# Moving the sine network of the Hyena filters to the head of the program, under raised priority

## The chip, the core and the metric

The kernel runs on one core of a Trainium2 chip. Five engines work side by side, each through its own list of instructions in a fixed order: PE (TensorE, matrix products), DVE (VectorE) and POOL (GpSimd) for element-wise work, ACT (ScalarE) for functions and copies, and SP (SyncE), which here only issues DMA transfers. The metric is the time of one execution on the device in microseconds (us), the median of several.

## The reference

One step of a two-layer model for 1024 tokens of a sample and 128 tokens of a prompt, 1024 channels wide. Layer 0 is a Hyena layer: a norm, shift and scale from a conditioning vector (adaLN), an input projection into x0, x1, v and a gate, a short convolution, a long convolution by Fourier transforms, an output projection. Layer 1 is latent attention with 16 heads. What the change touches is the small network that makes the filters of the long convolution:

```python
def hyena_filters(L, w1, b1, freq, w2, b2, w3):
    ...
    hdn = jnp.sin(fr * (z @ w1.astype(f32) + b1.astype(f32)))
    hdn = jnp.sin(fr * (hdn @ w2.astype(f32) + b2.astype(f32)))
    h = hdn @ w3.astype(f32)
    ...
    h = h * jnp.exp(-t * deltas)
    return h / jnp.sum(jnp.abs(h), axis=0, keepdims=True)
```

`z` depends on the position alone, and the hidden width is 64. So the two sine layers need nothing of the tokens, and the tokens need nothing of them until the filters are transformed. The rest that matters here:

```python
    hf = jnp.fft.rfft(filt, n=n, axis=0)
    ...
    y = jnp.fft.irfft(jnp.fft.rfft(z, n=n, axis=1) * hf, n=n, axis=1)[:, :L]
    y = (y + z * f_bias.astype(jnp.float32)).astype(h.dtype) * x0
    return (y * jax.nn.silu(gate)) @ w_out
```

## The kernel before, in words

Every float32 product is split into three with a high and a low part of each side (`_h`, `_l`), so a weight needs an ACT pass (`hi`, L86 to L93) and a POOL or DVE pass (`lo`, L94 to L96) before PE can use it.

The Hyena layer (`hyena`, from L654) runs in four stages.

1. **Start** (L680 to L739). Nine tiles of 128 tokens are loaded (`load_x`, L650), normed in thirds (squares L171 and root L172 on ACT, reciprocal L174 and scaling L176 on DVE), and turned by PE, three tiles at a time (`turn`, L178 to L182, 72 products of 128x128 into `sf_ps`, a tag with three PSUM buffers; ACT copies the result out at L700). Eight chunks of the adaLN weights, 1 MB each, go through PE (`ada_chunk`, L104 to L117) and are turned (`ada_turn`, L127). Then ACT applies shift and scale (`modulate`, L206), POOL and DVE split the result into `hT` and `lT` (L90, L96), and PE makes the first two of 30 blocks of the input projection in 144 products (L726), whose accumulators are three `ip_ps` and the three `sf_ps` buffers. The **sine network** (`filters`, L235 to L252) is written between the turning and these products. Its two layers (`sin_layer`, L211 to L225) each go in columns of 512, 512 and 128: a PE product into `sf_ps` (L215), a chain of seven DVE instructions that reduces the argument (L219 to L224), and the Sin on ACT (L225). The result is `hs`.
2. **Forward** (L740 to L762). For each of eight groups of 128 channels: the filter from `hs` (`group_filter`, L254), two blocks of the projection (`in_proj`, L404, 72 products each at L415), the short convolution (L435 to L443), the forward transform in PE products into `df_ps` (L357, L364, and L485 for the prompt) and the product with the filter, stored in DRAM. Between them lie 32 **chunks of the later adaLN weights** (`fill`, L753 to L755; four a group, L760), each in two halves with one buffer for the weights, turned at L127 or L142 and, for the gate rows, stored by POOL's queue (L146).
3. **Inverse** (L763 to L784). The inverse's constants `ic` and `ip` are loaded in the place that the filters' pool held, the pool of the weights of `fill` among it (`load_const`, L513 to L528, two buffers). Each group is read back, split (`pi_h` on ACT, `pi_l` on POOL), inverted by PE into `iv_ps` (L551), copied out by ACT (L553), put together by DVE (`ds`, `bf`, `yv`, L559 to L591) and stored (L784). Blocks of the projection that are left, for x0 and the gate, lie between (`PLAN`).
4. **Output** (from L785): the weights of `w_out` are loaded in the place of the constants, the eight results are read back (`y<-YD`, L792), split, and multiplied (L627).

The order on each engine is made by a scheduler from the written order: an instruction gets a priority by its place in the text, `urgent()` (L389) raises it by 3000 places, and of those that the scheduler's own model holds ready, the one of highest priority is put next. The lists are then fixed: an engine waits at the head of its list, even if later work is ready. The lines in question:

```python
                with self.urgent():
                    xs = [self.load_x(np_, t, NT + 1) for t in range(NT)]
                ...
                if FIRST == 1:
                    self.filters(fp, ps, hs)
                ...
                    with self.urgent():
                        for f in fill[4 * g:4 * g + 4]:
                            f()
```

Of the kernel before, what the change touches and what calls it, by code (L numbers as in the profile page):

```python
# [19 lines left out]
# channel groups whose x0 and gate are made along with a group's forward transform  # L20
GATES = (0, None, None, 1, None, None, None, None)
NY = 6          # channel groups inverted before the input projection ends
# [9 lines left out]
FIRST = 1  # L32
# [10 lines left out]
# the steps of a unit of attention (scores of the next one, transposes, products with the values)  # L43
# [10 lines left out]
NT = 9          # token tiles: 8 of the sample, 1 of the prompt  # L54
T = NT * P
EPS = 1e-6
# [13 lines left out]
# columns of the per-partition vector table  # L70
NK = 1408       # keys: 1024 of the sample, 256 of the cache, 128 of the prompt
# [4 lines left out]
class K:  # L76
# [8 lines left out]
    # hi = x rounded to float32r, lo = the exact rest  # L85
# [18 lines left out]
    # ---------------------------------------------------------------- adaLN  # L104
    def ada_chunk(self, layer, o, n, pool, ps, kk, bufs):
        """n columns from o of silu(cond) @ ada_w, as four partial sums on rows 32g + cond."""
# [12 lines left out]
    def ada_col(self, layer, m, o, n, pool, ps, kk, bufs):  # L119
        """columns o.. of shift and scale with the channel on the partition."""  # L120
        self.ada_turn(layer, m, o, n, self.ada_chunk(layer, o, n, pool, ps, kk, bufs), ps)
# [10 lines left out]
    def ada_mod(self, layer, m, A, k):  # L132
        """A = norm_w (1 + scale) for the channel tiles k."""
        c = C_NORM + 8 * layer
        nw = self.cols[:, c + k.start:c + k.stop].unsqueeze(2).broadcast_to([P, k.stop - k.start, 2])
        self.stt(A[:, k], m[:, 8 + k.start:8 + k.stop, :], 1.0, nw, ALU.mult, ALU.add)

    def ada_row(self, layer, gd, o, n, pool, ps, kk, bufs):
        """columns o.. of the gates as rows in DRAM."""
# [13 lines left out]
    # ------------------------------------------------- RMSNorm and modulate  # L153
# [11 lines left out]
    def norm(self, xs, ys, pool, eng=None):  # L165
        """ys = rmsnorm(xs) without its weight; the squares pass through ys, or a tile of their own."""
# [17 lines left out]
    def norm_mod(self, xs, tiles, pool, ps, A, B, hT, lT):  # L184
        """h^T (hi, lo): [128 channels, 8, tokens] of rmsnorm(x) * A + B, for neighbouring token tiles."""
# [12 lines left out]
    def modulate(self, x, k, c, pool, A, B):  # L198
        """x^T A + B for the channels k of the third c of the tokens."""
# [10 lines left out]
    # ------------------------------------------------------------- filters  # L210
    def sin_layer(self, pool, ps, w, src, kk, out, col):  # L211
        """out = sin(freq * (w^T src + b)) with the argument reduced to [-pi, pi]."""
# [14 lines left out]
    def load_w3(self, pool, g, bufs):  # L227
        """the last filter weights of 128 channels, forward and backward, on both halves of the rows."""
# [6 lines left out]
    def filters(self, pool, ps, hs):  # L235
        """hs: hidden features [hi; lo] by token."""
# [16 lines left out]
    # -------------------------------------------------------- long convolution  # L253
    def group_filter(self, g, q):  # L254
        """time-domain filter of 128 channels into the filter columns of E and O, and of the prompt."""
# [10 lines left out]
        # forward and backward taps: the sample at 0, the prompt at 1025, a zero behind each  # L266
# [9 lines left out]
        # the taps over the sums of their absolute values  # L276
# [11 lines left out]
        # sum and difference of the forward taps and the reversed backward ones  # L288
# [55 lines left out]
    def dft_tile(self, k0, ab, q):  # L344
        """the frequencies k0 + 16 m of z (columns 0:128) and of the filter (128:256)."""
# [22 lines left out]
    def product(self, pt, special, q, out):  # L368
        """out [128, 2, 128] = z * filter; special: row 0 holds two real frequencies."""
# [18 lines left out]
    # ------------------------------------------------------------ Hyena: in  # L388
# [15 lines left out]
    def in_proj(self, m, q, cb):  # L404
        """128 output channels of h @ hy_w_in; cb(psum, token offset)."""
# [16 lines left out]
    def conv_in(self, m, q):  # L422
        """one of x0, x1, v: projection, then the short convolution; [128, 1153] with column 1024 unused."""
# [21 lines left out]
    def hyena_group(self, g, q):  # L445
# [21 lines left out]
        # sample  # L467
# [7 lines left out]
        # prompt  # L475
# [54 lines left out]
    # ----------------------------------------------------------- Hyena: out  # L530
    def inverse(self, g, q):
        """y = irfft(product): [128 channels, T]."""
        nc, pool, ps = self.nc, q["pool"], q["ps"]
        ih, il, jh, jl = q["ih"], q["il"], q["jh"], q["jl"]
        # blocks 1 2 3 7 6 5 of (real, imaginary), and the blocks 0 (even, odd) and 4
# [22 lines left out]
        # d: W1 - W7, W2 - W6, W3 - W5 in blocks 0, 2, 4 (imaginary: 1, 3, 5), s: the sums in blocks 6..11  # L558
# [10 lines left out]
        # a0 a3 a2 a1 in blocks 0..3  # L569
# [22 lines left out]
        # prompt  # L592
# [17 lines left out]
    def load_w(self, src, pool, ncol, tag, bufs, raw_bufs=2, hi_eng="act", lo_eng="dve", lo_bufs=None, step=2, tag_raw="w_raw", size=None, stage=None):  # L610
        """a [128, kt, ncol] weight chunk, split."""
# [17 lines left out]
    # ------------------------------------------------------------------ run  # L629
# [25 lines left out]
    def hyena(self):  # L655
# [9 lines left out]
        # in thirds of the tokens: the first ones' place comes free before the last product ends  # L665
# [12 lines left out]
        with self.pool("hsp", side="right") as hp:  # L678
            hs = hp.tile([P, T], F32R, name="hs")
            q.update(hs=hs)  # L680
            with self.pool("fp", 2, side="right") as fp, self.pool("ap", side="right") as ap, \
# [3 lines left out]
                with self.urgent():  # L685
                    xs = [self.load_x(np_, t, NT + 1) for t in range(NT)]
                q["n"], q["w"] = 2, [self.in_weights(m, q) for m in q["order"][:2]]
                # the normed tokens with the channel on the partition: in places of the convolution's and of x
# [12 lines left out]
                if FIRST == 1:  # L701
                    self.filters(fp, ps, hs)
                # the first two projections, along the channels as they come
# [5 lines left out]
                # shift and scale of 256 channels at a time; a chunk is turned after the next one's products  # L709
# [19 lines left out]
                if FIRST == 2:  # L729
# [767 lines left out]
```

## Time and profile before

| | before |
|---|---|
| median of 3 runs | 1869.53 us (1867.89 to 1870.08) |
| profiled execution, first to last instruction | span 1868.4 us |
| PE busy | 1785.4 us (96%), 11480 products |
| DVE busy | 1291.5 us (69%) |
| ACT busy | 1116.4 us (60%) |
| POOL busy | 616.9 us (33%) |
| mean granted TensorE clock | 0.984 |
| DMA | 157.93 MB, mean 85 GB/s |

The profile has only the span of the profiled execution; the median is 1.1 us above it, and it is that execution's own time that the runs are compared by. Busy PE is not PE at its peak, since a product's end is modelled and overlaps the next one's start: distances between starts tell more. The shares are means over stages with different limits, so a stage is read by windows and by each engine's list in order of time.

### The profile page before, as it was taken

Reading aid. Unit: us, or ns where it says so; the run is one execution under the profiler, and the core shown is the slowest. Engines: PE = TensorE matmul, PEld = TensorE weight load, DVE = VectorE, ACT = ScalarE, POOL = GpSimd, SP = SyncE. Lnnn points to the kernel's source line nnn. Section 1 sums busy time; section 2 is a strip of 40 time slices with the busy share of each in tenths; the row PEclk is TensorE's granted clock in tenths of the full one; section 3 lists DMA queues with packets and bytes.
Section 4 is the critical chain, followed back from the end, with each engine's and each line's share of the span. In section 5 each row is a group of like instructions: output and inputs, shape, how many; then the busy total and the mean of one; then the engine's idle time right before and its main releaser. Section 6 shows DMA issues by size and latency. Waiting matters only on the chain.

```text
span 1868.4 us, 31762 instructions
## 1 busy us (share of the span) xinstructions
PE 1785.4 (96%) x11480; PEld 1585.0 (85%) x11480; DVE 1291.5 (69%) x2556; ACT 1116.4 (60%) x2650; POOL 616.9 (33%) x796
## 2 busy tenths in 40 slices
PE   6998999999999977999999989999999999999998
PEld 4887888887888877788999979999899998998786
DVE  3847887888865699753233268877887888778454
ACT  7655566665653443434353368878887888788431
POOL 2334433344345574233000042424343342235100
PEclk9999999999999988999999989999999999999999
DMA  8222232222223553731313410101010000012541
GB/s 316 83 84 72 66 94 93 82 82 66 74 95 112 168 167 103 279 134 65 94 33 109 102 31 19 42 16 46 20 37 28 20 28 24 18 35 62 180 134 68
DMA packets 126500, 157.93 MB, mean 85 GB/s; under 512 B 12711, under 2 KB 99687, under 8 KB 125064
## 3 DMA queue, kind: packets, MB, share of 16 engines
q1 hardware_dynamic: 123280, 152.51, 25.3%
q10 hardware_dynamic: 2552, 3.39, 0.6%
q8 instruction: 90, 1.47, 0.3%
q14 instruction: 66, 0.54, 0.1%
q0 software_dynamic: 512, 0.02, 0.0%
HBM read 113.89 MB, written 36.73 MB: 81 GB/s over the span
## 4 chain that ended last, share of the span: by engine, by line
PE 51%; DVE 5%; DMA 2%; ACT 1%; SPq 1%; issue 1%; POOL 0%; DVEq 0%; ACTq 0%; POOLq 0%
PE wo_ps L627 18%; PE wo_ps L1289 11%; PE av_ps L1174 8%; PE nm_ps L1162 7%; PE wo_ps L991 4%; PE nm_ps L1023 1%; DVE mx L1292 1%; DVE bf L99 1%; DMA og_in<-og 1%; SPq L978 1%; DMA y<-YD 0%; DVE kT L96 0%; PE nm_ps L842 0%; DMA wm_raw<-wm_a 0%; DVE yv L102 0%
## 5 line engine op out<-in xcount | busy, mean ns | idle before, releaser
L1289 PE MATMUL wo_ps<-kT,qT 128*128 128x512 f32 (+1 forms) x1152 | 281.4, 375 | 11.0 <-POOL qT L90 6.5
L1296 ACT ACTIVATE prob<-wo_ps,mx 128x512 f32<-128x512 f32 (+1 forms) x384 | 234.1, 618 | 22.9 <-DVE mx L1294 20.8
L1292 DVE TENSOR_REDUCE mx<-wo_ps 128x1 f32<-128x512 f32 (+1 forms) x384 | 213.0, 596 | 32.8 <-PE wo_ps L1289 32.1
L88 ACT ACTIVATE pt_h<-nm_ps 128x512 fp32r<-128x512 f32 x324 | 192.8, 599 | 70.4 <-PE nm_ps L1162 62.4
L1289 PEld LDWEIGHTS wo_ps<-kT,qT 128*128 128x128 f32 x1152 | 189.1, 191 | 46.4 <-ACT prob L1296 14.5
L96 DVE TENSOR_TENSOR pt_l<-nm_ps,pt_h 128x512 fp32r<-128x512 f32 x324 | 210.6, 683 | 13.0 <-ACT pt_h L88 12.8
L1162 PE MATMUL nm_ps<-ident,prob 128*128 128x128 f32 x1280 | 191.5, 272 | 0.0
L96 POOL TENSOR_TENSOR wi_l<-wi_raw,wi_h 128x512 fp32r<-128x512 f32 x64 | 127.3, 1989 | 185.1 <-ACT wi_h L88 181.7
L1162 PEld LDWEIGHTS nm_ps<-ident,prob 128*128 128x128 f32 x1280 | 150.0, 140 | 8.5
L415 PE MATMUL ip_ps<-lT,wi_h 128*128 128x384 f32 x720 | 157.1, 346 | 0.0
L415 PE MATMUL ip_ps<-hT,wi_l 128*128 128x384 f32 x720 | 152.8, 344 | 0.0
L415 PE MATMUL ip_ps<-hT,wi_h 128*128 128x384 f32 x720 | 152.5, 346 | 0.0
L1174 PE MATMUL av_ps<-pt_h,Vt 128*128 128x256 f32 x640 | 138.1, 297 | 0.0
L1174 PE MATMUL av_ps<-pt_l,Vt 128*128 128x256 f32 x640 | 135.4, 293 | 0.4 <-DVE pt_l L96 0.4
L415 PEld LDWEIGHTS ip_ps<-lT,wi_h 128*128 128x128 f32 x720 | 128.3, 192 | 6.7 <-issue 4.4
L415 PEld LDWEIGHTS ip_ps<-hT,wi_h 128*128 128x128 f32 x720 | 126.0, 190 | 6.4 <-issue 4.4
L415 PEld LDWEIGHTS ip_ps<-hT,wi_l 128*128 128x128 f32 x720 | 125.2, 189 | 7.1 <-issue 4.7
L627 PE MATMUL wo_ps<-wm_h,lhh 128*128 128x256 f32 (+1 forms) x432 | 126.5, 296 | 2.3 <-ACT wm_h L88 2.2
L1186 POOL TENSOR_SCALAR gt<-gt,sm 128x64 f32<-128x64 f32 x128 | 54.9, 443 | 220.6 <-DVE sm L1177 219.3
L627 PE MATMUL wo_ps<-wm_l,lhh 128*128 128x256 f32 (+1 forms) x432 | 127.1, 295 | 0.0
L627 PE MATMUL wo_ps<-wm_h,lhl 128*128 128x256 f32 (+1 forms) x432 | 126.7, 295 | 0.0
L99 POOL TENSOR_TENSOR pr<-ev 128x256 f32<-128x256 f32 x72 | 79.2, 1102 | 129.9 <-ACT ev L372 78.7
(354 smaller groups left out, 4348.2 us busy)
## 6 DMA issues: line engine op xcount, KB each, us to landing
wi_raw<-w_in SPq DMA_DIRECT2D x64, 256.0 KB, 3.0
ada_w<-ada_w SPq DMA_DIRECT2D x64, 256.0 KB, 2.8
x_in<-xs SPq DMA_DIRECT2D x16, 512.0 KB, 5.3
ada_w<-ada_w SPq DMA_DIRECT2D x8, 1024.0 KB
PS<-pr_o SPq DMA_DIRECT2D x64, 128.0 KB, 2.5
pi_raw<-PS SPq DMA_DIRECT2D x32, 256.0 KB, 3.6
YD<-yv SPq DMA_DIRECT2D x8, 576.0 KB, 4.5
y<-YD SPq DMA_DIRECT2D x8, 576.0 KB
```

The lines of the kernel that those rows point to most:

```text
L88: self.S.activation(out, src, AF.Copy)
L96: e.tensor_tensor(out, src, hi.bitcast(F32), ALU.subtract)
L99: (eng or self.V).tensor_tensor(out, x, y, op)
L415: mm = self.PE.matmul(pt, w[:, k, :], x[c][:, k, :], start=s == 0 and k == 0, stop=s == 2 and k == 7)
L627: self.PE.matmul(pt, x[k][:, sl], w[:, k, :], start=s == 0 and k == 0, stop=s == 2 and k == kt - 1)
L991: self.PE.matmul(pt[:, :n], x[:, k, o:o + P], y[:, k, c], start=s == 0 and k == 0, stop=s == 2 and k == kt - 1)
L1162: self.PE.transpose(pt[:, P * i:P * i + P], u["p"][i % 2][n // 2][:, P * (2 * (n % 2) + i // 2):P * (2 * (n % 2) + i // 2) + P], self.ident)
L1174: self.PE.matmul(u["po"][:, :256], m["V"][:, 2 * n + e, j, :], u[n][1 + s][:, 256 * e:256 * e + 256], start=n == first and e + s == 0, sto ...
L1186: self.G.tensor_scalar(o, o, u["sm"][:, i, 3:4], None, ALU.mult)
L1289: self.PE.matmul(pt[:, :n], x[:, j, P * i:P * i + P], y[:, j, o:o + n], start=s == 0, stop=s == 2)
L1292: self.V.tensor_reduce(mx[:, b:b + 1], c["s", i, b][:, :n], AX.X, ALU.max)
L1296: self.S.activation(c["p"][i][b], c["s", i, b][:, :n], AF.Exp, bias=c["mx"][i][:, 3:4], accum_out=c["sm"][:, i, b:b + 1])
```

## The change

`filters` is called first in the start stage, ahead of the token loads, and under `urgent()`; the call between the turning and the first products is taken out. Nothing that is computed changes. The comments and docstrings are taken out of the file too, which shifts line numbers by one to three (L726 before is L725 now) and leaves the program as it is.

```diff
-FIRST = 1
...
                 m0 = self.small.tile([P, 16, 2], F32, name="ada_m0")
                 with self.urgent():
+                    self.filters(fp, ps, hs)
+                with self.urgent():
                     xs = [self.load_x(np_, t, NT + 1) for t in range(NT)]
...
-                if FIRST == 1:
-                    self.filters(fp, ps, hs)
...
-                if FIRST == 2:
-                    self.filters(fp, ps, hs)
```

The scheduler makes other lists of it, down to the start of the output stage. Three places of them follow.

**PE at the start.** `zt`, `w` and `h` are the sine network's input, weights and first layer, `x_in` the tokens. Before:

```order
L181 MATMUL sf_ps<-ident,x_in 128x128 x33
L113 MATMUL ada_ps<-ada_w,cond 32x256 x8
L181 MATMUL sf_ps<-ident,x_in 128x128 x9
L113 MATMUL ada_ps<-ada_w,cond 32x256 x8
L127 MATMUL ada_ps<-sel,ada_ev 128x2 x2
L181 MATMUL sf_ps<-ident,x_in 128x128 x12
```

And now:

```order
L214 MATMUL sf_ps<-zt,w_150 64x512 x2
L214 MATMUL sf_ps<-zt,w_150 64x128
L214 MATMUL sf_ps<-h_156,w_152 64x512 x2
L214 MATMUL sf_ps<-h_156,w_152 64x128
L180 MATMUL sf_ps<-ident,x_in 128x128 x6
L112 MATMUL ada_ps<-ada_w,cond 32x256 x8
```

All six products of the network stand ahead of the first turning, those of the second layer among them, which need the first layer's sines.

**ACT at the start.** `nm_j` are the squares of a token tile, `nm_ss` the root, `cv<-sf_ps` the copy of turned tokens. Before:

```order
L171 ACTIVATE nm_j,nm_ss<-x_in 128x1024 x3
L172 ACT_TABLE_LOAD
L172 ACTIVATE nm_ss<-nm_ss,eps 128x3
L171 ACTIVATE nm_j,nm_ss<-x_in 128x1024 x2
L700 COPY cv<-sf_ps 128x384
```

And now:

```order
L170 ACTIVATE nm_j,nm_ss<-x_in 128x1024 x3
L224 ACTIVATE h_156<-mlp_x 64x512
L171 ACT_TABLE_LOAD
L171 ACTIVATE nm_ss<-nm_ss,eps 128x3
L170 ACTIVATE nm_j,nm_ss<-x_in 128x1024 x3
L87 ACTIVATE wi_h<-wi_raw 128x512
L171 ACTIVATE nm_ss<-nm_ss,eps 128x3
L224 ACT_TABLE_LOAD
L224 ACTIVATE h_156<-mlp_x 64x512
L170 ACTIVATE nm_j,nm_ss<-x_in 128x1024 x3
L224 ACTIVATE h_156<-mlp_x 64x128
L171 ACT_TABLE_LOAD
```

The first layer's three sines (L224) stand between the squares and roots of the norm, and the table is changed back and forth.

**PE behind the last product of the forward transform** (`df_ps`, of the prompt). `ip_ps` are blocks of the input projection, `ada_ps<-ada_w` the halves of a chunk of `fill`, `ada_ps<-ada_ev,sel` its turn. Before:

```order
L485 MATMUL df_ps<-sp_h,fc_l 128x128
L415 MATMUL ip_ps<-hT_123,wi_h 128x384 x6
L415 MATMUL ip_ps<-lT_124,wi_h 128x384
L113 MATMUL ada_ps<-ada_w,cond 32x128 x4
L415 MATMUL ip_ps<-lT_124,wi_h 128x384 x7
L415 MATMUL ip_ps<-hT_123,wi_l 128x384 x8
L415 MATMUL ip_ps<-hT_125,wi_l 128x384 x8
L415 MATMUL ip_ps<-lT_126,wi_h 128x384 x7
L113 MATMUL ada_ps<-ada_w,cond 32x128 x4
```

And now:

```order
L484 MATMUL df_ps<-sp_h,fc_l 128x128
L414 MATMUL ip_ps<-lT_122,wi_h 128x384 x2
L414 MATMUL ip_ps<-hT_121,wi_l 128x384 x8
L414 MATMUL ip_ps<-hT_123,wi_h 128x384 x8
L414 MATMUL ip_ps<-lT_124,wi_h 128x384 x5
L112 MATMUL ada_ps<-ada_w,cond 32x128 x4
L414 MATMUL ip_ps<-lT_124,wi_h 128x384 x3
L414 MATMUL ip_ps<-hT_123,wi_l 128x384 x8
L414 MATMUL ip_ps<-hT_125,wi_l 128x384 x8
L414 MATMUL ip_ps<-lT_126,wi_h 128x384 x8
L414 MATMUL ip_ps<-hT_125,wi_h 128x384 x3
L112 MATMUL ada_ps<-ada_w,cond 32x128 x4
```

and further down that list, past this chunk's turn:

```order
L112 MATMUL ada_ps<-ada_w,cond 32x128 x4
L414 MATMUL ip_ps<-lT_124,wi_h 128x384 x2
L414 MATMUL ip_ps<-hT_123,wi_l 128x384 x8
L414 MATMUL ip_ps<-hT_125,wi_l 128x384 x8
L414 MATMUL ip_ps<-lT_126,wi_h 128x384 x8
L414 MATMUL ip_ps<-hT_125,wi_h 128x384 x5
L112 MATMUL ada_ps<-ada_w,cond 32x128 x4
L414 MATMUL ip_ps<-hT_125,wi_h 128x384 x3
L414 MATMUL ip_ps<-hT_121,wi_h 128x384 x8
L414 MATMUL ip_ps<-lT_122,wi_h 128x384 x8
L414 MATMUL ip_ps<-hT_121,wi_l 128x384 x2
L141 MATMUL ada_ps<-ada_ev,sel 2x128
```

Before, one chunk of `fill` is left when the forward transform ends; now two are. Counted over PE's whole list, 1740 of the 2160 projection products (L415) stand ahead of the last chunk's turn before, and 1818 now; 1807 stand ahead of the first product of the inverse (`iv_ps`) before, and 1875 now; behind the last product of the inverse there are 122 before, and 29 now. All products of the forward transform and of `fill` stand ahead of the first of the inverse in both.

## Rows read from the trace of the kernel before

**Rows 1.** Windows: busy us (instructions) of PE, PEld, DVE, ACT, POOL; clock; DMA share; GB/s.

```profile
177.60:184.00 6.40, 6.36 (x26) 5.36 (x27) 4.23 (x8) 5.10 (x13) 3.02 (x3) 0.54 0.34 102
184.00:450.00 266.00, 265.97 (x1655) 227.87 (x1654) 222.08 (x463) 167.42 (x356) 103.94 (x71) 1.00 0.26 82
635.60:753.10 117.50, 92.88 (x585) 90.55 (x584) 116.60 (x178) 42.37 (x87) 66.97 (x37) 0.88 0.40 126
753.10:773.00 19.90, 16.32 (x84) 14.27 (x82) 14.56 (x11) 9.22 (x15) 7.32 (x3) 1.00 0.97 352
```

**Rows 2.** PE in order of time, start stage: start us, us, what, [idle before, releaser].

```profile
14.62 3.27 PE L181 MATMUL sf_ps<-ident,x_in 128*128 128x128 f32 x12 [14.62 <-DVE x_in L176]
28.87 1.64 PE L181 MATMUL sf_ps<-ident,x_in 128*128 128x128 f32 x12
38.13 1.07 PE L215 MATMUL sf_ps<-zt,w 33*64 33x512 f32 x2
...
59.23 0.43 PE L215 MATMUL sf_ps<-h,w 64*64 64x128 f32 x2
...
76.18 1.55 PE L415 MATMUL ip_ps<-hT,wi_h 128*128 128x384 f32 x8
```

**Rows 3.** ACT and its DMA queue in order of time, start stage.

```profile
3.87 1.28 ACT L646 ACT_TABLE_LOAD   x1 [3.87 <-DMA cols<-cols]
...
4.51 0.60 ACTq L245 DMA_DIRECT2D fcol<-f_cols  x1
...
7.83 1.06 ACT L171 ACTIVATE nm_j<-x_in 128x1024 f32<-128x1024 f32 x1 [1.40 <-DMA x_in<-xs]
...
11.97 1.28 ACT L172 ACT_TABLE_LOAD   x1
13.26 0.30 ACT L172 ACTIVATE nm_ss<-nm_ss,eps 128x3 f32<-128x3 f32 x1
...
49.21 0.63 ACT L225 ACTIVATE h<-mlp_x 64x512 f32<-64x512 f32 x1
```

**Rows 4.** DVE by line and form, 0 to 82 us: xcount | busy us, mean ns.

```profile
L102 DVE SCALAR_TENSOR_TENSOR mlp_x<-mlp_q,mlp_x 64x512 f32<-64x512 f32 x12 | 9.1, 754 | 0.0
L219 DVE TENSOR_SCALAR mlp_x<-sf_ps,fcol 64x512 f32<-64x512 f32 x4 | 3.2, 798 | 0.6 <-PE sf_ps L215 0.6
L221 DVE TENSOR_SCALAR mlp_q<-mlp_q 64x512 f32<-64x512 f32 x4 | 1.7, 418 | 0.1
```

**Rows 5.** PE in order of time, 590 to 612 us.

```profile
596.27 2.94 PE L415 MATMUL ip_ps<-hT,wi_h 128*128 128x384 f32 x16
599.04 0.86 PE L415 MATMUL ip_ps<-lT,wi_h 128*128 128x384 f32 x4
...
611.87 0.28 PE L551 MATMUL iv_ps<-ic_h,pi_h 128*128 128x256 f32 x1
```

**Rows 6.** SP's queue in order of time, first load of the inverse's constants.

```profile
602.78 0.94 SPq L516 DMA_DIRECT2D cst<-ic  x2
```

**Rows 7.** DVE in order of time, inverse stage.

```profile
635.60 3.72 DVE L99 TENSOR_TENSOR ds<-W 128x768 f32<-128x768 f32 x2 [1.47 <-ACT W L553]
...
734.12 1.43 DVE L99 TENSOR_TENSOR cv<-cv 128x1024 f32<-128x1024 f32 x2
735.46 0.76 DVE L99 TENSOR_TENSOR bf<-Z 128x256 f32<-128x256 f32 x2
```

**Rows 8.** Critical chain, 740 to 800 us: start us, us, what.

```profile
773.01 16.61 PE wo_ps L627 x70
```

**Rows 9.** PE in order of time, the two long stalls of the forward stage.

```profile
177.64 0.65 PE L113 MATMUL ada_ps<-ada_w,cond 128*32 128x128 f32 x8 [4.67 <-DMA ada_w<-ada_w]
...
459.28 0.51 PE L364 MATMUL df_ps<-ab_hi,fc_h 128*128 128x512 f32 x1 [3.92 <-ACT ab_hi L88]
```

**Rows 10.** DVE and POOL by line and form, 635.6 to 753.1 us.

```profile
L99 DVE TENSOR_TENSOR bf<-Z 128x256 f32<-128x256 f32 x14 | 18.4, 1358 | 0.3
L96 POOL TENSOR_TENSOR wi_l<-wi_raw,wi_h 128x512 fp32r<-128x512 f32 x5 | 9.9, 1980 | 8.2 <-ACT wi_h L88 8.2
```

## The prediction

> **What bounds the kernel now.** I read the profile in this order: windows over the span, to see which engine is full in which stage; each engine's list in the first 80 us, where the moved work lies; then PE's list at the ends of the stages, because a list that is in a fixed order hands on whatever it has lost.
>
> The windows show two regimes [rows 1]. In the forward stage PE has no gap: 265.97 of 266.00 us between 184 and 450. There, a microsecond of PE is a microsecond of the kernel, and DVE (222 of 266) and ACT cost nothing. In the inverse stage, from 635.6 to 753.1, DVE is busy 116.6 of 117.5 us and PE 92.9: DVE bounds. What follows, up to 773, is a chain of transfers (DMA share 0.97) that needs the last inverse's result. In the critical chain PE has its next long run from 773.01 on, in the output products [rows 8], and all that lies behind is in the same order in both kernels. So the time follows two dates: when DVE can begin its chain of the inverse, at 635.60 [rows 7], and how long that chain is.
>
> At the start PE waits 14.62 us for the first normed tokens [rows 2]. It then turns tokens, pushes the first chunks of adaLN weights through and makes the first two blocks; the sine network's products lie between them, from 38.13 to 59.23. The first block of the next kind starts at 76.18.
>
> **The change, part by part.**
>
> *The network's products leave PE's full stretch.* Four of 512 columns take 1.07 us, two of 128 take 0.43 [rows 2]: 4 x 1.07 + 2 x 0.43 = 5.1 us, and the place that they go to, the first 14.62 us, is empty. That is the gain, if the turning still starts at 14.62.
>
> *It doesn't.* The new list has all six products ahead of the first turning, so PE now waits for the whole first layer. The steps: `fcol`, which the first DVE step needs, is issued at 4.51 and takes 0.60 to issue. The very first load was waited for until 3.87, so it took no longer than that; `fcol` lands between 5.1 and 4.51 + 0.60 + 3.87 = 9.0. I take 8.0, since token tiles are landing at that time (first use at 7.83) [rows 3]. DVE needs for a piece of 512 columns one instruction of 0.80, three of 0.42 and three of 0.75 us, 4.3 us; with the next piece's first one in between, 5.1 us [rows 4]. These are means of busy time that overlap their neighbours a little; I take 4.8, so 12.8. Then ACT, in its new order: sine 0.63, table 1.28 and root 0.30 [rows 3], to 15.0; three squares of 1.2 each, the 1.06 of the row and the read of the sum, to 18.6; the weights' `hi` pass (512 columns too, so about 0.6), a root, a table, a sine, to 21.4; three squares to 25.0; the short sine 0.3. With PE's last product of 0.43 the turning starts at about 25.7, between 23 (`fcol` at 5.1) and 27: 11.1 us later than 14.62.
>
> From there PE has the work of the old stretch without the network: 76.18 - 14.62 - 5.1 = 56.5 us, less what the old stretch lost at its beginning and the new one doesn't. The first 12 turnings took 3.27 us, the later ones 1.64 for 12 [rows 2]: 33 of them at the difference of 0.14 is 4.5 us at most, and 0 if the first ones are slow again. I take 3.0, as by then tokens have landed and norms are done for two thirds, so that PE meets fewer waits. 25.7 + 56.5 - 3.0 = 79.2: the forward stage starts **3.0 us later** (bounds -1 and +6). DVE's 20 us of sine work leave 40 to 75 us, where PE was full anyway, and are worth nothing there. The filters are ready some 35 us earlier, and nothing waited for them.
>
> *Two more table loads.* The new ACT list changes the table three times before the first turning, the old one once. A load takes 1.28 us and the root starts at 13.26, 1.29 after the load began [rows 3]; these are in the steps above. The Trainium skill, "ScalarE: Activation LUTs", section "What ACT_TABLE_LOAD costs", adds a drain of about 1.38 us to each switch, 2.66 in all. By that the start would be an estimated 3 x 1.38 = 4.1 us later still and the time 1888.3; the row shows no such gap, so I don't take it.
>
> *The end of the forward stage.* The same 32 chunks of the later adaLN weights are placed otherwise among the products. Before, one chunk is left behind the last forward transform, now two. PE is full there, so the list is the clock: 68 more projection products (1875 against 1807) stand ahead of the first product of the inverse, each 2.77 / 16 = 0.173 us (596.27 to 599.04) [rows 5]: **11.8 us**. By the last chunk's turn it is 78 products (1818 against 1740), 13.5 us. That turn counts too: the constants of the inverse are loaded in the place of the pool that these chunks use, first at 602.78 [rows 6], 9.1 us ahead of the first inverse product at 611.87 [rows 5]; both move by about as much. I take 11.8; the other bound is 0, if DVE's chain could begin earlier than the constants and PE's order let it, which the fixed list excludes.
>
> *Those 68 products are not lost, but they lose their cover.* In the old list 122 of them, 122 x 0.173 = 21 us, fill PE behind the last inverse product, under the transfers of 753 to 773. Now 29 are left there, 5 us, and PE will idle while DMA does what it did. That idling is the price, in another place.
>
> *DVE's chain* itself gets one gate product more (1.43 us [rows 7]), and POOL has one weight split fewer (mean 1.98 [rows 10]) to share time with it: 0 together, bounds -2 and +3.
>
> **Sum:** 3.0 + 11.8 + 0 = 14.8 us. The profiled execution spans 1868.4, so 1883.2; the median of the runs stands 1.1 above that span: **1884.3 us**, 0.8% slower.
>
> **Rivals.**
>
> *The stalls of the old forward stage go away.* PE had two long ones: 4.67 us for adaLN weights and 3.92 us for ACT [rows 9], and after the first the granted clock is 0.54, near the 1.2 of 2.4 GHz, for 6.4 us [rows 1], which costs 6.4 x 0.46 = 2.9. Together 11.5 us. Both are collisions of the order, and the new order may not have them: 1884.3 - 11.5 = 1872.8, no change that can be told (a measurement of this kernel tells about 0.2%, 3.7 us). Against it: nothing in the new list takes away what they come from, one weight buffer for `fill` and SP's list behind POOL's, and it can have stalls of its own. 13%.
>
> *Faster, by DVE and POOL in the inverse stage.* The instruction `bf<-Z` takes 0.38 us when alone (0.76 for two [rows 7]) and 1.36 on average over 14 [rows 10], and POOL is busy 67 of these 117.5 us [rows 1]. So a good part of the bounding chain is time lost beside POOL, and how the two meet depends on the order. The Trainium skill, "GPSIMD Engine Reference", section "Key points", says that POOL shares its SBUF interfaces with DVE where DVE has two inputs in SBUF; the trace agrees (1.36 against 0.38). If a third of POOL's 67 us stopped being paid, 22 us, the time would be 1862, faster. It decides from 18.5 us on (14.8 and the 3.7 of the bound). For it: 14 x 0.98 = 13.7 us are lost in that one group. Against it: POOL has the same splits to make from the same loads, and its list in this stage differs by one instruction. 10%.
>
> *Worse than forecast.* `fcol` late, or a new stall of the size of the old ones with its slow clock (7.6 us): 1884.3 + 8 = 1892. This lies in the forecast's own range.
>
> **How the numbers follow.** The forecast, slower with its two terms, gets 77%, no change 13%, faster 10%. Its own bounds: 3.0 from -1 to +6, 11.8 to 13.5, the chain -2 to +3, stalls from half gone (-6) to one more (+8): 1873 to 1898. The range for 8 in 10 takes in the first rival at the lower end and leaves out the second: 1868 to 1897. Slower 0.77, same 0.13, faster 0.10.
>
> **What would show it.** Right: PE's first turning near 25 us instead of 14.62, with the network's six products ahead of it and ACT's table loads between the squares; the first block at L414 near 79; the first product of the inverse 10 to 18 us later than 611.87; DVE full from then for about 117 us; PE with some 15 us of gaps just ahead of the output products, which start as much later as the inverse did. Wrong: the first turning at 15 to 17, or the first inverse product at 612 or earlier with no more projection products ahead of it, or DVE's chain below 100 us.

## The result, and the profile after

The changed kernel takes **1886.76 us** in the median of four executions (1885.96 to 1893.15), the kernel before 1869.80 (1867.89 to 1872.04) beside it: a ratio of 1.0095, with an interval of 1.0077 to 1.0113. It is 17 us slower; 1884.3 was forecast, 14.8 us slower.

The profiled execution is the longest of the four (1893.15, span 1891.1), so a second profile of the same kernel, run e1 below (span 1884.9), is read beside it.

In order of time, PE of the changed kernel from the start to the first long stalls (start us, us, what, [idle before, releaser]):

```profile
4.26 4.07 PE L214 MATMUL sf_ps<-zt,w 33*64 33x512 f32 x6 [4.26 <-DMA w<-f_w]
16.16 1.97 PE L214 MATMUL sf_ps<-h,w 64*64 64x512 f32 x2 [7.83 <-ACT h L224]
23.82 1.96 PE L214 MATMUL sf_ps<-h,w 64*64 64x512 f32 x2 [5.69 <-ACT h L224]
27.42 0.69 PE L214 MATMUL sf_ps<-h,w 64*64 64x128 f32 x2 [1.64 <-ACT h L224]
28.04 1.54 PE L180 MATMUL sf_ps<-ident,x_in 128*128 128x128 f32 x6
29.51 1.94 PE L112 MATMUL ada_ps<-ada_w,cond 128*32 128x256 f32 x16
31.37 1.08 PE L180 MATMUL sf_ps<-ident,x_in 128*128 128x128 f32 x6
32.39 1.07 PE L112 MATMUL ada_ps<-ada_w,cond 128*32 128x256 f32 x16
...
77.51 1.55 PE L414 MATMUL ip_ps<-hT,wi_h 128*128 128x384 f32 x8
82.39 1.12 PE L414 MATMUL ip_ps<-hT,wi_h 128*128 128x384 f32 x4 [2.64 <-ACT wi_h L87]
...
172.09 0.66 PE L112 MATMUL ada_ps<-ada_w,cond 128*32 128x128 f32 x8 [7.46 <-DMA ada_w<-ada_w]
```

The network's products stand in the hole ahead of the first turning, and PE waits three times for a sine. The turning starts at 28.04, 13.4 us later than before [rows 2], and the next kind of block at 77.51, only 1.3 later. DVE and ACT ahead of the turning:

```profile
10.53 0.80 DVE L218 TENSOR_SCALAR mlp_x<-sf_ps,fcol 64x512 f32<-64x512 f32 x1 [9.38 <-DMA fcol<-f_cols]
```

```profile
15.48 0.63 ACT L224 ACTIVATE h<-mlp_x 64x512 f32<-64x512 f32 x1 [3.66 <-DVE mlp_x L223]
16.12 1.28 ACT L171 ACT_TABLE_LOAD   x1
17.42 0.30 ACT L171 ACTIVATE nm_ss<-nm_ss,eps 128x3 f32<-128x3 f32 x1
...
21.84 1.28 ACT L224 ACT_TABLE_LOAD   x1
...
27.39 1.28 ACT L171 ACT_TABLE_LOAD   x1
```

`fcol` came at 10.5, the sine was done at 16.11, and the three table loads are there; the third, at 27.39, stands behind the last sine, so no turning waits for it. The end of the forward stage on PE, SP and DVE, which answers to [rows 5 to 7]:

```profile
592.36 0.27 PE L484 MATMUL df_ps<-sp_h,fc_l 128*128 128x128 f32 x1
621.06 0.38 PE L141 MATMUL ada_ps<-ada_ev,sel 128*2 128x128 f32 x2
631.37 0.28 PE L550 MATMUL iv_ps<-ic_h,pi_h 128*128 128x256 f32 x1
...
789.05 0.80 PE L626 MATMUL wo_ps<-wo_h,lhh 128*128 128x512 f32 x1 [21.09 <-POOL lhh L89]
```

```profile
620.89 0.90 SPq L515 DMA_DIRECT2D cst<-ic  x2
```

```profile
660.17 3.76 DVE L98 TENSOR_TENSOR ds<-W 128x768 f32<-128x768 f32 x2 [1.42 <-ACT W L552]
```

And windows of the inverse stage and of what follows (busy us and instructions of PE, PEld, DVE, ACT, POOL; clock; DMA share; GB/s), which answer to [rows 1]:

```profile
660.20:776.30 116.10, 88.86 (x548) 85.66 (x546) 114.81 (x179) 38.57 (x82) 58.58 (x34) 0.87 0.37 120
776.30:797.00 20.70, 7.95 (x26) 6.32 (x27) 8.52 (x9) 8.74 (x11) 6.89 (x3) 0.60 0.97 350
```

DVE's chain starts 24.6 us later than before and is as full and nearly as long (114.8 of 116.1 us). Then PE idles for 21.09 us, where before it had projection products and then, in the output products, three short waits:

```profile
764.92 0.50 PE L627 MATMUL wo_ps<-wo_h,lhh 128*128 128x512 f32 x1 [1.40 <-POOL lhh L90]
768.50 0.50 PE L627 MATMUL wo_ps<-wo_h,lhl 128*128 128x512 f32 x1 [1.45 <-POOL lhl L96]
773.01 0.50 PE L627 MATMUL wo_ps<-wo_h,lhl 128*128 128x512 f32 x1 [0.74 <-DVE lhl L96]
```

In e1 the same dates are 28.25 for the turning, 589.30 for the last forward transform, 628.30 for the first inverse product, 655.40 for `ds`, 784.58 for the first output product.

### The profile page after: what moved, and what is told of

Same layout as the page of the kernel before. It is cut to its first block, busy times and chain, and to the rows that moved or that the text cites. A ratio compares the mean times of both kernels' runs of the same rounds, so it can differ in the third digit from the quotient of the medians.

```text
span 1891.1 us, 31760 instructions
## 1 busy us (share of the span) xinstructions
PE 1788.0 (95%) x11480; PEld 1589.6 (84%) x11480; DVE 1283.8 (68%) x2556; ACT 1120.2 (59%) x2652; POOL 596.9 (32%) x796
## 4 chain that ended last, share of the span: by engine, by line
PE 51%; DVE 3%; DMA 2%; ACT 1%; SPq 1%; issue 1%; POOL 0%; DVEq 0%; ACTq 0%; POOLq 0%
PE wo_ps L626 18%; PE wo_ps L1286 11%; PE av_ps L1171 8%; PE nm_ps L1159 7%; PE wo_ps L988 4%; PE nm_ps L1020 1%; DVE mx L1289 1%; SPq L975 1%; DMA og_in<-og 1%; DMA wm_raw<-wm_a 0%; PE nm_ps L839 0%; DMA y<-YD 0%; PE nm_ps L180 0%; DVE kT L95 0%; PE av_ps L1208 0%
## 5 line engine op out<-in xcount | busy, mean ns | idle before, releaser
L1286 PEld LDWEIGHTS wo_ps<-kT,qT 128*128 128x128 f32 x1152 | 190.0, 191 | 44.7 <-ACT prob L1293 12.8
L95 DVE TENSOR_TENSOR pt_l<-nm_ps,pt_h 128x512 fp32r<-128x512 f32 x324 | 210.4, 682 | 13.0 <-ACT pt_h L87 12.8
L95 POOL TENSOR_TENSOR wi_l<-wi_raw,wi_h 128x512 fp32r<-128x512 f32 x64 | 115.1, 1798 | 200.3 <-ACT wi_h L87 200.3
L414 PE MATMUL ip_ps<-hT,wi_h 128*128 128x384 f32 x720 | 158.4, 349 | 2.6 <-ACT wi_h L87 2.6
## 6 DMA issues: line engine op xcount, KB each, us to landing
ada_w<-ada_w SPq DMA_DIRECT2D x8, 1024.0 KB, 13.5
```

The costliest lines, as they stand in the source:

```text
L95: e.tensor_tensor(out, src, hi.bitcast(F32), ALU.subtract)
L414: mm = self.PE.matmul(pt, w[:, k, :], x[c][:, k, :], start=s == 0 and k == 0, stop=s == 2 and k == 7)
L1286: self.PE.matmul(pt[:, :n], x[:, j, P * i:P * i + P], y[:, j, o:o + n], start=s == 0, stop=s == 2)
```

## The experiments

All twelve runs in one table, with the kernel before and the changed one. The dates are those of the profiled execution: the last product of the forward transform, the first of the inverse, and `ds`, the first step of DVE's chain. The projection products between the first two dates are counted in PE's list. Ratios below are to the kernel before as it ran beside each: a median of 1868.48 us with e1 to e4, 1868.99 with e5 to e8, 1870.25 with e9 to e12.

| run | median us | last forward | first inverse | distance | products between | x 0.173 | ds | span - ds |
|---|---|---|---|---|---|---|---|---|
| before | 1869.80 | 588.32 | 611.87 | 23.6 | 125 | 21.6 | 635.60 | 1232.8 |
| after | 1886.76 | 592.36 | 631.37 | 39.0 | 205 | 35.5 | 660.17 | 1230.9 |
| e1 | 1888.68 | 589.30 | 628.30 | 39.0 | 205 | 35.5 | 655.40 | 1229.5 |
| e2 | 1863.84 | 588.65 | 599.73 | 11.1 | 63 | 10.9 | 626.59 | 1237.3 |
| e3 | 1874.43 | 590.91 | 610.74 | 19.8 | 104 | 18.0 | 636.56 | 1236.0 |
| e4 | 1907.74 | 607.60 | 652.39 | 44.8 | 223 | 38.6 | 678.46 | 1230.8 |
| e5 | 1880.77 | 581.48 | 617.09 | 35.6 | 185 | 32.0 | 642.76 | 1230.4 |
| e6 | 1881.32 | 588.66 | 619.96 | 31.3 | 170 | 29.4 | 645.71 | 1233.4 |
| e7 | 1881.32 | 585.18 | 619.29 | 34.1 | 180 | 31.1 | 649.37 | 1233.3 |
| e8 | 1866.92 | 581.25 | 602.62 | 21.4 | 116 | 20.1 | 631.92 | 1232.8 |
| e9 | 1883.26 | 591.77 | 631.30 | 39.5 | 208 | 36.0 | 650.02 | 1232.6 |
| e10 | 1864.00 | 589.63 | 601.24 | 11.6 | 66 | 11.4 | 615.96 | 1248.5 |
| e11 | 1869.95 | 587.80 | 611.80 | 24.0 | 128 | 22.1 | 631.44 | 1236.5 |
| e12 | 1873.27 | 585.46 | 616.09 | 30.6 | 160 | 27.7 | 641.91 | 1230.0 |

Two things hold in it. The distance from the last forward transform to the first inverse product is the count of products at 0.173 us, and what is left over, 0.2 us to 6.2, goes with the chunks of `fill` that stand there too: 0.2 without one, 2.0 with one, 3.5 with two, most with e4's. And from `ds` on each profiled execution takes 1229 to 1237 us, but for e10. Most of these 8 us lie in DVE's chain itself: from `ds` to its last `yv` it took 117.5 us before, 116.1 in the changed kernel, and 119.1 to 123.6 in e2, e6 and e8 to e11, whose edits brought `ds` forward. The first output product came 11.9 to 13.1 us behind that `yv` in every order but e10's (19.4). So a `ds` that comes earlier was worth less there than its distance.

### e1: the changed kernel again

No edit.

> The changed kernel once more, to see which of its stalls belong to its lists. In its first profile PE lost 7.46 us at 172 to a chunk of adaLN weights, 3.04 us at 241 and 2.64 us at 82, and that execution was 6.3 us above the three others. Theory (lists): time 1886 to 1888, first turning near 28, the first product of the inverse 15 to 20 us later than 611.87, DVE's chain of the inverse some 116 us long, as before. Rival (stalls): the 17 us are stalls of the forward stage; then the stall near 172 comes again with 7 us or more and PE's gaps between 60 and 600 us add up to over 20.

1888.68 us (ratio to before 1.0098, 1.0079 to 1.0116). The stalls at 82 (2.92) and 172 (7.38) come again and so belong to the lists; the one of 3.04 at 241 does not come. Gaps of 0.4 us or more add up to 12.8 us between 60 us and the first inverse product, 9.1 before: the rival's 20 are not there. What stands behind the long one, on POOL, SP and PE:

```profile
157.32 11.16 POOL L95 TENSOR_TENSOR wi_l<-wi_raw,wi_h 128x512 fp32r<-128x512 f32 x1
```

```profile
168.52 0.34 SPq L398 DMA_DIRECT2D wi_raw<-w_in  x1
168.96 0.38 SPq L109 DMA_DIRECT2D ada_w<-ada_w  x1
```

```profile
172.44 0.65 PE L112 MATMUL ada_ps<-ada_w,cond 128*32 128x128 f32 x8 [7.38 <-DMA ada_w<-ada_w]
```

One split of weights on POOL takes 11.16 us (the next, at 172.28, takes 1.28). SP's list has the next `wi_raw`, which needs its buffer, ahead of the chunk's `ada_w`, so `ada_w` goes out at 168.96 and PE waits for it. DVE was busy 10.04 of the 11.16 us meanwhile, and idle during the 1.28. The Trainium skill, "GPSIMD Engine Reference", section "Key points", says that POOL shares its SBUF interfaces with DVE where DVE has two inputs in SBUF; the trace agrees, with 11.16 against 1.28.

### e2 and e3: quarters of a chunk in two buffers

```diff
-FK, FB = 4, 1
+FK, FB = 2, 2
```

e2 is the changed kernel with this edit, e3 the kernel before.

> The change, with the weights of the later adaLN chunks in quarters of 2 row tiles and two buffers, in place of halves of 4 and one buffer (same room). The order that comes of it has 1769 projection products ahead of the first inverse product in place of 1875 and no chunk behind the last forward transform. Theory (lists): 106 x 0.173 = 18.3 us less than the changed kernel, 1868.5; the start as in the changed kernel, turning at 28. Rival (stalls, the start): what is lost is lost at the start and to stalls, the tail doesn't matter, and twice as many loads on SP make more of them: 1887 or more.

> The same quarters with two buffers in the kernel before: 1763 products ahead of the first inverse product in place of 1807. Theory (lists): 44 x 0.173 = 7.6 us less than before, 1862; against the run above it then differs by the start alone, 3 us, and 6 products, 1 us. Rival (stalls, the start): no gain, 1869 or more.

e2: 1863.84 us, **faster than both kernels**, by 0.3% in the case of the one before (ratio to before 0.9969, 0.9956 to 0.9983). The gain is 23 us on the changed kernel, 18.3 were expected: its distance falls from 39.0 to 11.1 us, and the stall at 172 is gone too (one gap of 2.65 us in all the forward stage). Of the 28.8 us by which `ds` came earlier than in e1, 7.8 were lost behind it, most of them in DVE's chain (121.2 us in place of 116.1). e3: 1874.43 (1.0035, 1.0020 to 1.0049), slower than before, where 1862 was expected. Its distance fell as it should, from 23.6 to 19.8, but the last forward transform came 2.6 us later, in spite of 23 products fewer ahead of it (4.0 us): the gaps are 12.2 us in place of 9.1, and the chunks' products from 85 to 585 us were busy for 29.7 us in place of the 26.6 shown under e4. Behind `ds` it took 3.2 us more.

```profile
L113 PE MATMUL ada_ps<-ada_w,cond 128*32 128x128 f32 x496 | 29.7, 287 | 3.2 <-DMA ada_w<-ada_w 3.2
```

So a count from the head of the list is worth its time only if the stalls stay, and they don't.

### e4: eighths of a chunk in four buffers, in the kernel before

```diff
-FK, FB = 4, 1
+FK, FB = 1, 4
```

> The kernel before with eighths of a chunk in four buffers: its start is unchanged, but the order has 1887 products ahead of the first inverse product in place of 1807, and two chunks behind the last forward transform, as the changed kernel has. Theory (lists): 80 x 0.173 = 13.8 us more than before, 1883.6, with PE's first turning at 14.6 and the network at its old place. Rival (the start costs the time): 1870, as the start is the old one.

1907.74 us (1.0203, 1.0186 to 1.0220): slower with the old start, but by 39 us and not 14. PE had no gap of 0.4 us or more between 60 us and the first inverse product, and yet its last forward transform came 19.3 us late. The lines of the chunks' products from 85 to 585 us (xcount | busy us, mean ns | idle before) tell why, first of the kernel before:

```profile
L113 PE MATMUL ada_ps<-ada_w,cond 128*32 128x128 f32 x496 | 26.6, 287 | 5.1 <-DMA ada_w<-ada_w 5.1
```

and of e4:

```profile
L113 PE MATMUL ada_ps<-ada_w,cond 128*32 128x128 f32 x456 | 52.2, 285 | 0.0
```

Fewer recorded products take twice the time, though one takes the same 285 ns: by these rows the products of a half, which stand in fours in PE's list, overlap more than those of an eighth, which stand alone. That it is because the code puts four partial sums on four groups of 32 rows is argued, not shown. The rest is the tail, 44.8 against 23.6. e4 doesn't settle the tail's price, as it changed another; e5 does.

### e5 and e6: one chunk more, one chunk less

e5, the kernel before with one chunk made twice:

```diff
+                fill += [fill[-1]]
...
-                        for f in fill[4 * g:4 * g + 4]:
+                        for f in fill[4 * g:4 * g + 4 + (g == 7)]:
```

> The kernel before, with the last of the 32 later adaLN chunks made twice. All of its order up to the last forward transform stays as it was, then two chunks follow in place of one, and 1867 projection products stand ahead of the first inverse product in place of 1807 (1875 in the changed kernel). Theory (tail): 60 x 0.173 = 10.4 us, and 1 to 2 us for the chunk's own products on PE: 11.9 us more than before, 1881. The first inverse product 12 us later than 611.87, and a gap of 15 to 21 us ahead of the output's products. Rival (the start and the stalls cost the time, the tail has slack): only the chunk's own products, 1870 to 1871.

e6, the changed kernel with one less:

```diff
+    def ada_bias(self, layer, gd, o, n, pool):
+        row = pool.tile([2, n], F32, name="ada_row", tag="ada_row", bufs=1)
+        self.nc.sync.dma_start(row, self.a["ada_gb"][layer:layer + 1, o:o + n].squeeze(0).partition_broadcast(2))
+        self.nc.gpsimd.dma_start(gd.squeeze(0)[:, o:o + n], row)
...
+                fill[31:] = [lambda o=o: self.ada_bias(1, gd[1], o, P, fpool) for o in range(7 * P, D, P)]
```

> The changed kernel, with the last of the 32 chunks not computed (its rows of the gate are the bias alone). Its start and its forward stage stay as they are; one chunk is left behind the last forward transform, as before the change, and 1840 products ahead of the first inverse product in place of 1875. Theory (tail): 35 x 0.173 = 6.1 and 1 to 2 for the chunk's products, 7.6 us less than the changed kernel, 1879; by the last chunk's turn (1744 in place of 1818 products) it would be 12.8 and 1.5, 1873. Rival (the start and the stalls): 1885 to 1887.

e5: 1880.77 us (1873.30 to 1883.06; ratio 1.0055, 1.0034 to 1.0076), against 1881 by the tail and 1870 by the rival. Its profiled execution was one of the shorter (1875.46), as the stall of 3.92 us at 459 of [rows 9] isn't in it, but its own tail is:

```profile
581.48 0.27 PE L485 MATMUL df_ps<-sp_h,fc_l 128*128 128x128 f32 x1
592.99 0.38 PE L142 MATMUL ada_ps<-ada_ev,sel 128*2 128x128 f32 x2
607.29 0.38 PE L142 MATMUL ada_ps<-ada_ev,sel 128*2 128x128 f32 x2
617.09 0.28 PE L551 MATMUL iv_ps<-ic_h,pi_h 128*128 128x256 f32 x1
```

Two chunks are turned behind the last forward transform, and the distance is 35.6 us in place of 23.6: 12.0 more, 11.9 were expected. Ahead of the output's products PE has a gap of 20.03 us, as in the changed kernel. e6: 1881.32 (1.0073, 1.0044 to 1.0102), against 1.0095 and 1.0098 for the changed kernel, so 4 to 5 us less, where 7.6 were expected and 0 to 2 by the rival. Its distance is 31.3 in place of 39.0, 7.7 less; behind `ds` it took 1233.4 us, 3.9 more than e1, with a chain of 119.3. From both sides: **a chunk that is left at the end costs its place in the list, and the start is not needed for it.**

### e7 and e8: the network behind the first third's turning

e7 is the kernel before with this edit; e8 has `FK, FB = 2, 2` too.

```diff
+                    if c == 0:
+                        self.filters(fp, ps, hs)
-                if FIRST == 1:
-                    self.filters(fp, ps, hs)
```

> The network at a third place: written behind the turning of the first third of the tokens, without raised priority. No turning waits for a sine, so PE's first turning is at 14.6 again, and the lists differ from both kernels: 1816 products ahead of the first inverse product (before 1807, changed 1875), one and a half chunks behind the last forward transform. Theory (tail and start): 9 x 0.173 = 1.6 us more than before, 1870 to 1871. Rival (any earlier network costs, as its sines and DVE steps delay the norms and turnings): as much as the changed kernel, 1880 or more.

> The same third place, with the quarters of a chunk in two buffers. 1744 products ahead of the first inverse product, 25 fewer than in the changed kernel with quarters (1863.8 us). Theory (tail and start): 25 x 0.173 = 4.3 us less for the tail and up to 4 less for the start, 1856 to 1860. Rival (the gain of the quarters hangs on whether the long stall near 172 us goes away, which it did with the network at the head and did not with the network at its old place): with the stall 1868 or more.

e7: 1881.32 us (1.0065, 1.0040 to 1.0090). The theory's 1870 fell, and the rival's number came, though not for its reason: PE's first turning is at 14.68 and PE has next to no gap from 22 to 60 us. But its products take nearly twice their time (PE, then the window of 20 to 30 us; what its clock column, 1.00, is worth is said in the last section):

```profile
26.21 3.64 PE L113 MATMUL ada_ps<-ada_w,cond 128*32 128x256 f32 x32
47.32 1.94 PE L113 MATMUL ada_ps<-ada_w,cond 128*32 128x256 f32 x16
54.40 1.15 PE L113 MATMUL ada_ps<-ada_w,cond 128*32 128x256 f32 x16
57.05 1.07 PE L113 MATMUL ada_ps<-ada_w,cond 128*32 128x256 f32 x16
```

```profile
20.00:30.00 10.00, 9.30 (x46) 3.55 (x45) 8.26 (x15) 5.27 (x13) 0.68 (x1) 1.00 0.72 283
```

1.94 against 1.07 us for the same 16 products, up to 54 us, and the first projection block of the next kind starts at 85.41, 9.2 us later than before. And the tail has 180 products in place of 125 (10.5 us more, as measured), and `ds` came 30.1 us behind the first inverse product, 23.7 before: my count of 9 from the head had hidden that the forward transform ended 46 products earlier in the list. e8: 1866.92 (1.0001, 0.9988 to 1.0014), not the 1856 to 1860 expected: its products are as slow in stretches until 46 us, 6.3 us of gaps are left, and its tail is 10.3 us longer than e2's. Still, the quarters are worth 12 us by these two ratios.

### e9, e10, e11: a third buffer for the inverse's constants

```diff
-                ih, il = self.load_const(pc, "ic", 512 + 7 * 384, pc, "cst", 256, nc.sync)
-                jh, jl = self.load_const(pool, "ip", 256, pc, "cst", 256, nc.sync)
+                ih, il = self.load_const(pc, "ic", 512 + 7 * 384, pc, "cst", 256, nc.sync, 3)
+                jh, jl = self.load_const(pool, "ip", 256, pc, "cst", 256, nc.sync, 3)
```

In the changed kernel (e9), in e2's (e10) and in the kernel before (e11).

> The changed kernel with three buffers in place of two for the loads of the inverse's constants. DVE's first step of the inverse's chain (ds) came 27 to 29 us behind the first inverse product in the changed kernel and 23.7 before, and the 14 constants, one ahead of the other through two buffers, took 38 to 39 us from the first load to that step, 33 before. Theory (the constants' loads hold DVE's chain up): that distance falls to 33 or less, the chain starts 3 to 6 us earlier and the time is 1881 to 1884, with first turning, stalls and the last forward transform as in the changed kernel. Rival (PE's list sets the start of the chain): 1887, the distance stays.

> The changed kernel with quarters of a chunk (1863.8 us) and three buffers for the constants. There the last chunk is turned before the forward transform ends, and the constants took 42.8 us from the first load at 583.8 to ds at 626.6. Theory (the constants' loads): some 33 us from the first load, or as soon as PE's order lets it; 5 to 9 us less, 1855 to 1859, the fastest of all. Rival (PE's list): 1863 to 1865.

> The kernel before with three buffers for the constants; PE's count ahead of the first inverse product is 1810, before 1807. Theory (the constants' loads): the distance of 32.8 us shrinks here too, by 0 to 4 us, 1865 to 1869. Rival (PE's list): no change, 1869.

e9: 1883.26 us (1.0066, 1.0047 to 1.0086; 1881 to 1884 expected). From the first inverse product to `ds` it takes 18.7 us in place of 27.1 in e1, so the constants do hold DVE's chain up. Its chain is longer, 119.1 us. e10: 1864.00 (0.9963, 0.9950 to 0.9976), as e2 and not 1855 to 1859: `ds` moved by 10.6 us, from 626.59 to 615.96, and the whole of it was given back. The window from 732 us, when the next to last result is stored, to the first output product:

```profile
732.00:759.00 27.00, 27.00 (x158) 27.00 (x157) 17.81 (x30) 9.53 (x18) 7.54 (x4) 1.00 0.76 272
```

PE is full now. 205 projection products stand behind the last inverse product at 723.28 there, 205 x 0.173 = 35.5 us, and the first output product comes at 758.98. e11: 1869.95 (0.9999, 0.9988 to 1.0011); `ds` came 4.2 us earlier there and the time stayed, as DVE's chain took 122.5 us in place of 117.5 and ended later. Its last steps, before and in e11:

```profile
751.89 1.16 DVE L102 SCALAR_TENSOR_TENSOR yv<-bf,yv 128x128 f32<-128x128 f32 x4
```

```profile
752.83 1.15 DVE L102 SCALAR_TENSOR_TENSOR yv<-bf,yv 128x128 f32<-128x128 f32 x4
```

What made the chain longer there wasn't tried.

### e12: the first sine layer alone at the head

```diff
+                with self.urgent():
+                    self.filters(fp, ps, hs)
...
-                if FIRST == 1:
-                    self.filters(fp, ps, hs)
+                self.filters2(ps, hs)
```

`filters` ends behind its first layer, `filters2` does the rest.

> Only the first sine layer at the head, the second at the network's old place: no turning waits for a sine, though the first norm's scaling still stands behind DVE's steps of the layer, so PE's first turning comes at about 20.5 in place of 28. The tail stays nearly as in the changed kernel, 1866 products ahead of the first inverse product (changed 1875, before 1807). Theory (start and tail): the start costs 0 to 3 us in place of 4 to 6, the tail 59 x 0.173 = 10.2; 1879 to 1883. Rival (the late turning is what the change pays for): within 3 us of before, 1868 to 1872. Rival (the start costs nothing at all): 1886 to 1888.

1873.27 us (1.0012, 1.0000 to 1.0024), some 6 us below what was expected, and near the first rival. The tail is 7.0 us longer than before (160 products, 30.6 us) and not 10.2, as 24 of the 59 products stand ahead of the last forward transform; and with these ahead of it that transform still comes 2.9 us earlier than before. There is one gap of 2.26 us from 60 us on, none at 172. POOL's split is slow there too, but SP's list has `ada_w` ahead of the `wi_raw` that waits for it:

```profile
165.52 7.01 POOL L96 TENSOR_TENSOR wi_l<-wi_raw,wi_h 128x512 fp32r<-128x512 f32 x1 [4.77 <-ACT wi_h L88]
```

```profile
163.56 0.38 SPq L110 DMA_DIRECT2D ada_w<-ada_w  x1
...
172.56 0.33 SPq L403 DMA_DIRECT2D wi_raw<-w_in  x1
```

So whether the late turning costs isn't settled by e12, as its stalls went too: the first turning was at 18.82 in place of 28.04, and the gap at 83 came all the same.

## Why the prediction was right

- **The end of the forward stage** (11.8 us by the first inverse product, 13.5 by the last turn) was the main term, and it holds. From the last forward transform to the first inverse product it took 15.4 us more (39.0 against 23.6): 80 products more, 13.8 us, and one more chunk, whose own products the sum left out. 12 of the 80 stood ahead of that transform before, which gives the 68 of the forecast. e5 and e6, one chunk more and one less, show it by 12.0 and 7.7 us of distance; of the time it was 10 to 12 us in e5 and 4 to 5 in e6.
- **The start** (3.0 us, bounds -1 and +6) came to 1.3 at the first block of the next kind and 4.0 with the wait of 2.64 us for `wi_h` at 82, which wasn't foreseen. The first turning was forecast at 25.7, at most 27, and came at 28.04: `fcol`'s step of DVE began at 10.53, not at 8.0, beyond the bound of 9.0. From there on the steps took what was worked out: 4.95 us to the sine (4.8) and 12.6 to the turning (12.9). That it mattered so little was rightly seen, for a reason that was half right: the turnings were fast 3 us after their start and not 11 [rows 2], as the granted clock had risen by then (last section).
- **The table loads**: the row shows a sine ending at 16.11, the load from 16.12 and the root at 17.42. The Trainium skill, "ScalarE: Activation LUTs", section "What ACT_TABLE_LOAD costs", adds a drain of 1.38 us; the trace doesn't show it, and it was rightly left out. Its price was also mis-counted: only two of the three loads stand ahead of the last sine, so by that page it is an estimated 2.8 us and not 4.1.
- **The constants "move by about as much"**: their first load and the first inverse product did (18.1 and 19.5 us, 15.1 and 16.4 in e1). The step that failed is the next one, that DVE's chain moves with them. From the first inverse product to `ds` it took 28.8 us, 27.1 in e1, against 23.7: 3.4 to 5.1 us that the sum doesn't have. e9 shows that the 14 constants through two buffers set this distance in the changed kernel; why they took 37.6 to 39.3 us from the first load to `ds` there, and 32.8 before, is not shown.
- **The lost cover**: a gap of 21.09 us (20.46 in e1) ahead of the output's products, some 15 expected. But the first output products met three waits of 1.40, 1.45 and 0.74 us before, at 764.92, 768.50 and 773.01, and none now, so that 3 us came back behind it.
- **DVE's chain** (0, from -2 to +3): 116.1 us against 117.5.
- **The bounds**, added up as they stand, give 1872 to 1900 and not 1873 to 1898; nothing hangs on it.

By dates, with e1, whose execution is near the median: the first inverse product comes 16.4 us later (14.8 forecast), `ds` 19.8, the last `yv` 18.4, the first output product 19.7, the end 16.5. So the mechanism is the forecast's up to the first inverse product, but that the total came within 2 us is in part luck: behind it 4.6 us that the sum doesn't have (3.4 and 1.3) were offset by 4.6 others (1.4 in the chain, 3.2 in the output's waits).

**The rivals.** The stalls of the old forward stage did not go away: the one at 172 came in place of that at 177 [rows 9], with 7.4 us in place of 4.7, from the same queue. The 3.92 us at 459 went, and others came, 12.8 us of gaps in all against 9.1. e2 and e12 show that an order without the long ones exists; in e12 the forward transform ended 7.1 us earlier than its count of products would have it, of the 11.5 that the rival had. The change doesn't have such an order. DVE's chain next to POOL kept its length within 1.4 us, and the faster case fell with it. That the priority itself does something was never a term: the lists of all five engines come out the same if the network stands first without it, and the same as before if it is raised at its old place.

## What to carry to other kernels

Moving work into an idle start can lengthen a list somewhere else: compare the two orders at the ends of the stages, where a fixed list hands on what it has lost, and price the difference by the start-to-start distance of the products. Look there for a paced side job with one buffer (here `fill`): two smaller buffers were worth 23 us in the changed order and 12 in e7's, and cost 6 in the old one. A count of the list prices a tail well, and a whole stage only as long as its stalls stay where they were.

## What the runs showed of the hardware

- PE's first products took nearly twice their later time (16 adaLN products 1.94 us, then 1.07), though the column of the clock reads 1.00 in those windows. The trace's list of granted levels begins only later, with the upper of the two levels, 2.4 GHz: at 26.4 us in the kernel before, 31.8 in the changed one, 54.6 in e7. The column counts the time ahead of that as 1.00. In e8 the first entry is at 29.5, and a later stretch reads 0.50, the lower level of 1.2 GHz; there the same row takes 1.94 us again:

```profile
30.41 1.07 PE L113 MATMUL ada_ps<-ada_w,cond 128*32 128x256 f32 x16
40.07 1.94 PE L113 MATMUL ada_ps<-ada_w,cond 128*32 128x256 f32 x16
```

```profile
36.30:46.50 10.20, 9.89 (x44) 4.93 (x48) 7.00 (x19) 3.40 (x9) 0.52 (x2) 0.50 0.84 322
```

  So ahead of the first entry the durations tell the clock, and the column doesn't. In the changed kernel the upper level came 3.8 us after the first turning, in the kernel before 11.8, in e7 39.9, though PE was busy there without a gap from 22 us on. What brings it on wasn't tried.
- Products of 32 columns for adaLN took 26.6 us as halves of a chunk and 52.2 as eighths (e4), at 287 and 285 ns each: the mean of one instruction said nothing of what a group costs.
- Executions of one kernel differ by up to 14 us here (the kernel before beside e5 to e8, 1860.66 to 1874.48), and a single stall of 3 us that comes in one profile and not in another of the same lists (at 241 in the changed kernel, 3.04 us, not in e1) can be a part of that.
